# A gated ConvFFN inside a two-layer diffusion backbone: a second tile for the gate chunk, weight sums made in place, a fourth raw buffer, and smaller pieces around them

## The chip, the cores and the metric

The kernel runs on one core of a Trainium2 chip. The metric is the device time of one execution in microseconds (us), lower is better. The kernel before takes 3467.93 us in the median of two runs (3467.13 and 3468.74).

## The reference, cut to what matters

One sequence of 1024 latent tokens (width 1024) and 256 context tokens goes through two layers: differential attention, then neighbourhood attention on a 16 x 64 grid, each followed by the same gated feed-forward block with a three-point convolution along the tokens (D_FF is 2816). Scale, shift and gate of each block come from a modulation matrix `ada_w`. Layer 1 has no context output.

```python
def conv_ffn(t, w_up, w_conv, b_conv, w_down):
    u = t @ w_up                                   # (n, 1024) @ (1024, 5632)
    up = jnp.pad(u, ((0, 0), (1, 1), (0, 0)))
    acc = b_conv
    for tap in range(3):
        acc = acc + up[:, tap:tap + n] * w_conv[tap]
    a, g = jnp.split(acc, 2, axis=-1)
    return (jax.nn.silu(g) * a) @ w_down
...
x = x + g2 * conv_ffn(rmsnorm(x, norm_ffn[i]) * (1.0 + sc2) + sh2, ...)
```

## The kernel before

All large products are fp32 to near full accuracy from a reduced-precision matmul format: every operand is split into a high part and a low remainder, and a product is high x high + high x low + low x high, three matmuls per 128 x 128 block of weights. A weight split is a cast on ScalarE for the high part and a subtraction on GpSimd (POOL) or VectorE (DVE) for the low one.

`Weights` (L75 to L205) is one stream of weight blocks in the order in which the kernel consumes them. It loads raw fp32 tiles of [128, 1024] into a ring of `RAW` = 3 buffers (pool `raw3`, L1141 to L1145), splits them (cast L138, subtraction L142; `high_low` L146 to L151 for weights that are built from others) and hands them out by `get`. SyncE (SP) issues all these DMAs in order.

The up projection of the FFN over the 1024 latent tokens uses a fast scheme with seven products for a 2 x 2 block product (token halves by weight halves), so it needs sums and differences of weight quarters a1, a2, g1, g2 (a and g are the value and gate columns of one chunk of 128 channels) and the token forms T1 to T4 and B22 (`token_forms`, L558 to L598). Each product is 12 matmuls of 512 columns.

- Pass 1 of layer 0 goes over the 22 chunks: the context product for a and g (48 matmuls of 256 columns), and for the first `ne` = 11 chunks also two latent products (`first`, `second`, L617 to L625). For these 11 the sums are built on POOL by `sums` (L180 to L190, four additions in place) and written to DRAM (`sscr`). The token forms are made meanwhile, two steps per chunk from chunk 2 on (loop L660). Layer 1 has no context; its pass 1 runs over 8 chunks.
- The main loop (L686 to L736) goes over all 22 chunks in the order of `SEQUENCE`: chunk ne + i, then chunk i, so 11 pairs in layer 0, and 8 pairs and 6 single chunks in layer 1. A chunk i >= ne is loaded by `pair` (L153) as raw a and g tiles, gets its sums in the loop by `halves` (L159 to L178, which here uses the pool `sum3`), and needs 7 products of 12 matmuls. A chunk i < ne reads its sums back from `sscr` and needs 5 products. So a pair is 144 matmuls.
- What follows each product in the loop is DVE and ScalarE work whose order is written out by hand (PE and DVE are on a manual schedule): additions of two products (L696, L700, L708, L715, L719) give the columns of a and g, ScalarE writes the middle tap (`centre`, L627), DVE adds the other taps (`tap`, L630), ScalarE applies Silu (L727), and `gated` (L730) multiplies and stores to `gscr`. Four such items of a chunk are put in a list `rest` and are run within the next chunk: tap of acc_g, the second tap with Silu, the two taps from `uh`, and gated. `while rest: fill()` before L708 empties the list. The gate chunk `ug` is one tile (`work[:, 3]`), so ug of the next chunk can't be written before acc_g has read it.

The down projection (`down`, L760 onward) runs three blocks of columns in layer 0 (at 0: context, 256 columns; at 1 and at 2: 512 columns each), 22 weight blocks k for each, eight output rows j. At a turn between blocks two weight blocks are taken first for all j (L783 to L797): six of the eight banks are free at once, and the norm of the block before is put in at j = 4 and j = 6. In layer 0 hooks add work beside it: `ada_rows` (L1226 to L1237) multiplies quarters of layer 1's modulation matrix by the conditioning vector on DVE, at the steps of `ADA_AT`; `ada_columns` (L1245) turns the rows by tiny matmuls; at the steps of `SUM_AT` `sums` builds the weight sums of layer 1.

## Time and profile before

| | us |
|---|---|
| median of the runs | 3467.93 |
| the profiled execution | 3468.82 |
| span of the trace of that execution | 3467.0 |
| layer 0 FFN: pass 1, first 11 and other 11 chunks | 156.9 and 63.2 |
| layer 0 FFN: 11 pairs | 439.8 |
| layer 0 FFN: down at 0 and the turn after it; at 1; turn; at 2 | 113.5; 105.9; 30.0; 143.5 |
| layer 1 FFN: pass 1; 8 pairs; 6 single chunks | 40.0; 327.7; 118.8 |
| layer 1 FFN: down of both blocks with the turn | 238.5 |

The span is what the trace covers; 1.8 us lie around it. The stages are windows of the trace cut at the matmuls that begin them. The rest of the span, about 1690 us, is attention and projections.

### The profile page before, as it was taken

Reading aid. Unit: us, or ns where it says so; the run is one execution under the profiler, and the core shown is the slowest. Engines: PE = TensorE matmul, PEld = TensorE weight load, DVE = VectorE, ACT = ScalarE, POOL = GpSimd, SP = SyncE. Lnnn points to the kernel's source line nnn. Section 1 sums busy time; section 2 is a strip of 40 time slices with the busy share of each in tenths; the row PEclk is TensorE's granted clock in tenths of the full one; section 3 lists DMA queues with packets and bytes.
Section 4 is the critical chain, followed back from the end, with each engine's and each line's share of the span. In section 5 each row is a group of like instructions: output and inputs, shape, how many; then the busy total and the mean of one; then the engine's idle time right before and its main releaser. Section 6 shows DMA issues by size and latency. Waiting matters only on the chain.

```text
span 3467.0 us, 43539 instructions
## 1 busy us (share of the span) xinstructions
PE 3192.5 (92%) x15632; PEld 2624.0 (76%) x15632; DVE 2130.6 (61%) x3294; ACT 1400.1 (40%) x2388; POOL 1730.6 (50%) x984
## 2 busy tenths in 40 slices
PE   8999889998998888888989979999999888889998
PEld 4888667776777877777867768888997677778876
DVE  6577488887467466666575344425994766676352
ACT  3111277775143543333423232225993433334111
POOL 2224166663347765555733641113662455678763
PEclk9999999998999999999989999999999999999999
DMA  7565344342445733333665667647873333334542
GB/s 258 161 220 172 107 110 107 111 116 88 152 139 182 216 117 104 116 113 112 231 210 177 213 221 236 224 150 175 197 193 125 123 111 113 109 107 157 196 156 70
DMA packets 253928, 536.82 MB, mean 155 GB/s; under 512 B 29584, under 2 KB 102160, under 8 KB 253712
## 3 DMA queue, kind: packets, MB, share of 16 engines
q1 hardware_dynamic: 252704, 533.72, 48.6%
q8 instruction: 124, 2.03, 0.3%
q14 instruction: 92, 0.75, 0.1%
q10 hardware_dynamic: 1008, 0.32, 0.0%
HBM read 395.24 MB, written 138.67 MB: 154 GB/s over the span
## 4 chain that ended last, share of the span: by engine, by line
PE 49%; POOL 16%; issue 13%; DVE 11%; DMA 8%; ACT 3%; SPq 0%; POOLq 0%; ACTq 0%; DVEq 0%
PE qk_ps L428 9%; PE w_ps L767 9%; POOL wsp L142 6%; PE w_ps L608 6%; POOL wf L151 4%; PE wo_ps L428 3%; PE o L1038 3%; PE sl L987 3%; PE o L1429 2%; PE v_ps L438 2%; PE v_ps L439 2%; PE v_ps L440 2%; PE tp L1014 2%; PE w_ps L428 1%; DMA raw<-in_down_dram 1%
## 5 line engine op out<-in xcount | busy, mean ns | idle before, releaser
L142 POOL TENSOR_TENSOR wsp<-raw,wsp 128x1024 fp32r<-128x1024 f32 (+2 forms) x285 | 647.9, 2281 | 716.6 <-ACT wsp L138 710.8
L767 PE MATMUL w_ps<-g,wsp 128*128 128x512 f32 (+1 forms) x2640 | 575.8, 380 | 50.1 <-POOL wsp L142 23.2
L767 PEld LDWEIGHTS w_ps<-g,wsp 128*128 128x128 f32 x2640 | 474.4, 195 | 150.1 <-POOL wsp L142 28.8
L138 ACT CAST wsp<-raw 128x1024 fp32r<-128x1024 f32 (+1 forms) x213 | 195.0, 928 | 365.1 <-PE w_ps L608 158.2
L608 PE MATMUL w_ps<-FT,wsp 128*128 128x512 f32 x912 | 253.8, 437 | 83.4 <-DVE work L708 58.7
L428 PE MATMUL qk_ps<-Hh,wsp 128*128 128x512 f32 x1280 | 319.7, 372 | 0.0
L140 POOL TENSOR_SCALAR wsp<-raw 128x1024 fp32r<-128x1024 f32 x72 | 99.8, 1388 | 397.4 <-DMA raw<-in_wqk_dram 144.8
L608 PEld LDWEIGHTS w_ps<-FT,wsp 128*128 128x128 f32 x912 | 190.4, 212 | 140.2 <-issue 97.5
L608 PE MATMUL w_ps<-FT,wf 128*128 128x512 f32 x1200 | 288.1, 392 | 4.4 <-DVE t L696 4.3
L608 PEld LDWEIGHTS w_ps<-FT,wf 128*128 128x128 f32 x1200 | 226.5, 189 | 53.9 <-DVE t L696 4.8
L555 DVE TENSOR_TENSOR g<-t,g 128x512 fp32r<-128x512 f32 (+1 forms) x102 | 135.8, 1372 | 211.6 <-ACT g L554 211.6
L428 PEld LDWEIGHTS qk_ps<-Hh,wsp 128*128 128x128 f32 x1280 | 215.3, 188 | 38.2
L630 DVE SCALAR_TENSOR_TENSOR work<-work,c_ffn_conv 128x1023 f32<-128x1023 f32 x88 | 170.9, 1943 | 98.1 <-ACT work L627 97.2
L994 ACT ACTIVATE E<-E,st 128x1280 f32<-128x1280 f32 x128 | 175.4, 1370 | 65.1 <-DVE st L989 64.1
L1004 POOL TENSOR_TENSOR E<-E,E 128x1280 f32<-128x1280 f32 x64 | 188.3, 2943 | 5.3
L608 PE MATMUL w_ps<-Hh,wsp 128*128 128x512 f32 x528 | 177.6, 402 | 8.4 <-ACT p L620 8.4
L1002 POOL TENSOR_SCALAR E<-E,st 128x1280 f32<-128x1280 f32 x64 | 85.6, 1337 | 193.4 <-DVE st L997 122.1
L989 DVE CUSTOM_DVE_ANT_0 E<-sl,zero,st 128x1024 f32<-128x1024 f32 x128 | 163.8, 1281 | 22.9 <-PE sl L987 22.2
L428 PE MATMUL qk_ps<-Hl,wsp 128*128 128x512 f32 (+1 forms) x640 | 175.3, 371 | 0.0
L1366 POOL TENSOR_SCALAR E<-E,st 128x640 f32<-128x640 f32 (+1 forms) x128 | 98.9, 774 | 149.9 <-PE s L1357 81.6
L987 PE MATMUL sl<-kst,q 128*128 128x512 f32 x512 | 160.0, 436 | 1.6 <-DVE st L989 1.5
L352 DVE SCALAR_TENSOR_TENSOR ada<-raw,c_cvec,ada 128x512 f32<-128x512 f32 x168 | 133.0, 827 | 41.2 <-DMA raw<-in_ada_w_dram 39.9
(606 smaller groups left out, 7011.7 us busy)
## 6 DMA issues: line engine op xcount, KB each, us to landing
raw<-in_down_dram SPq DMA_DIRECT2D x110, 512.0 KB
raw<-in_ada_w_dram SPq DMA_DIRECT2D x96, 512.0 KB
gscr<-work SPq DMA_DIRECT2D x44, 512.0 KB
t<-gscr SPq DMA_DIRECT2D x88, 256.0 KB
raw<-sscr SPq DMA_DIRECT2D x38, 512.0 KB
raw<-in_up_dram SPq DMA_DIRECT2D x33, 512.0 KB
raw<-in_wqk_dram SPq DMA_DIRECT2D x32, 512.0 KB
q<-qscr SPq DMA_DIRECT2D x256, 64.0 KB
```

What stands on the lines that cost most here:

```text
L138: nc.scalar.copy(out=sp[:, 0, c:c + n], in_=raw[:, c:c + n])
L142: nc.gpsimd.tensor_tensor(out=sp[:, 1, c:c + n], in0=raw[:, c:c + n], in1=f32(sp[:, 0, c:c + n]), op=ALU.subtract)
L151: nc.gpsimd.tensor_tensor(out=sp[:, 1, :], in0=src, in1=f32(sp[:, 0, :]), op=ALU.subtract)
L428: T.matmul(out=ps, lhsT=w[:, kc, :], rhs=H[b][s][:, kc, :], start=(kc == 0 and i == 0), stop=(kc == KC - 1 and i == 2))
L555: eng.tensor_tensor(out=form[:, kc, 1, :], in0=x, in1=f32(form[:, kc, 0, :]), op=ALU.subtract)
L608: T.matmul(out=ps, lhsT=w, rhs=form(kc, s), start=(start and kc + i == 0), stop=(kc == 3 and i == 2), skip_group_check=not start)
L630: stt(out=acc, in0=u, scalar=convw[:, l, c, k:k + 1], in1=acc, op0=ALU.mult, op1=ALU.add)
L767: T.matmul(out=ys[j][:, :n], lhsT=w[:, j, :], rhs=g[:, k % 4, s, :], start=(k == 0 and i == 0), stop=(k == NF - 1 and i == 2))
L987: T.matmul(out=ps[:, 512 * c:512 * c + 512], lhsT=qs[2 * j + s][:, qc], rhs=ks[j][:, 512 * c:512 * c + 512], start=(s == 0), stop=(s == 1))
L989: V.tensor_tensor_reduce(out=E[j][:, :SEQ], in0=ps, in1=zero.broadcast_to([P, SEQ]), op0=ALU.add, op1=ALU.min, scale=-1.0, scalar=m, accum ...
L994: S.activation(out=E[j], in_=E[j], func=AF.Exp, scale=-1.0, bias=m, accum_out=sm)
L1004: G.tensor_tensor(out=E[0], in0=E[0], in1=E[1], op=ALU.add)
```

## The change

`sums` and the forms of the chunks i >= ne now share one routine, `add_up`, that works in place in the two raw tiles: g2 is split first (`raw.append(self.high_low(g2, 512, False))`), then four additions turn the tiles into the four combinations, then the whole a tile and the whole g tile are split. The pool of the sum tile goes, and the raw ring gets a fourth buffer. The sums are written to DRAM as two tiles instead of four halves, and the main loop takes T1 and T3 from one weight tile, T2 and B22 from the other. `ug` alternates between two tiles, and the last item of `rest` (gated) is run after the addition that writes ug[hi]. Token forms advance one step per chunk in layer 0, and `second` with its copies stands ahead of them. The context product takes its bank from the six-bank pool. The quarters of `ada_w` no longer come through the weight stream: `ada_rows` loads them into a tile of its own, which has the name and the buffer of the second ug tile, and all 16 stand at (at 1, k = 3 to 18). At a turn three weight blocks are taken for j = 0 to 5 before j = 6 and 7. Small ones: `NP1` of layer 1 is 3 and `late` holds two; `R` has one buffer in the last phase; the split tiles of layer 1's q and k share one ring of three.

```diff
-NP1 = (2, 4)
-RAW = 3
+NP1 = (2, 3)
+RAW = 4
-ADA_AT = [(0, 6), (0, 12)] + [(1, k) for k in range(3, 17)]
-SUM_AT = [(2, k) for k in range(2, 18, 2)]
+ADA_AT = [(1, k) for k in range(3, 19)]
+SUM_AT = [(2, k) for k in range(3, 19, 2)]
...
         if i == 0:
-            raw.append(self.sum_pool.tile([P, 1024], F32, name=f"sum{self.count}", tag="sum"))
-            s = raw[2]
-            tt(out=s[:, 512:], in0=g1, in1=g2, op=ALU.add)
-            tt(out=s[:, :512], in0=s[:, 512:], in1=a1, op=ALU.subtract)
+            raw.append(self.high_low(g2, 512, False))
+            self.add_up(a1, a2, g1, g2)
+            self.high_low(ra, 1024)
         elif i == 1:
-            tt(out=a1, in0=a1, in1=g1, op=ALU.subtract)
-            tt(out=a2, in0=a2, in1=raw[2][:, :512], op=ALU.subtract)
-        self.high_low((raw[2], ra, g2)[i] if i < 2 else g2, (1024, 1024, 512)[i])
+            self.high_low(rg, 1024)
+        else:
+            self.made.append((raw[2], 0))
...
-                    gg, ps = W.get(), bank(1)
+                    gg, ps = W.get(), bank()
...
-                for _ in range((2, 99)[l]):
+                for _ in range((1, 99)[l]):
...
-        acc_g, ug = work[:, 2], work[:, 3]
+        acc_g, ug2 = work[:, 2], np_.tile([P, SEQ], F32, name="ug")
...
-                while rest:
+                while len(rest) > 1:
                     fill()
+                acc_a, uh, ug = work[:, at % 2], np_.tile([P, 514], F32, name="uh"), work[:, 3] if at % 2 else ug2
                 V.tensor_tensor(out=ug[:, hi], in0=y, in1=q, op=add)
-                acc_a, uh = work[:, at % 2], np_.tile([P, 514], F32, name="uh")
+                fill()
...
-                for j in range(KC):
-                    if b == 1 and j == 4:
-                        if turn:
-                            turn()
-                        chain = rnorm_steps(yp, np_, SS, 0, 512)
-                        next(chain)
-                    if j == 6:
-                        if b == 1:
-                            write(0, out_[0], next(chain))
-                        ys.extend(bank(1) for _ in range(2))
+                for j in range(6):
                     for k in range(2):
+                        down(k, j, sps[k])
+                if b == 1:
+                    if turn:
+                        turn()
+                    chain = rnorm_steps(yp, np_, SS, 0, 512)
+                    next(chain)
+                sps.append(W.get())
+                load_g(1)
+                for j in range(6):
+                    down(2, j, sps[2])
+                if b == 1:
+                    write(0, out_[0], next(chain))
+                ys.extend(bank(1) for _ in range(2))
+                for j in (6, 7):
+                    for k in range(3):
                         down(k, j, sps[k])
...
-                if l == 0 and (at, k) in ADA_AT:
-                    add_quarters(q1, 1)
...
-        t = W.get().rearrange("p (k n) -> p k n", k=2)
+        t = np_.tile([P, 1024], F32, name="ug")
+        nc.sync.dma_start(out=t, in_=a["ada_w"][1, n, k])
+        t = t.rearrange("p (k n) -> p k n", k=2)
```

ScalarE in the main loop, in the chunk that reads its sums back, before (raw154a, raw154g and sum154 belong to the chunk after it):

```order
L138 CAST wsp153_11938<-raw153_11936 128x1024
L627 ACTIVATE work_11126<-uh_11919,c_ffn_conv_74 128x512
L150 CAST wf154_11968<-sum154_11965 128x1024
L627 ACTIVATE work_11126<-work_11126,c_ffn_conv_74 128x1024
L727 ACTIVATE work_11126<-work_11126 128x1024
L150 CAST wf155_12006<-raw154a_11961 128x1024
L711 COPY uh_12026<-t_11958 128x1
L150 CAST wf156_12043<-raw154g_11962 128x512
L627 ACTIVATE work_11126<-uh_12026,c_ffn_conv_74 128x512
```

The same place in the changed kernel:

```order
L138 CAST wsp153_11910<-raw153_11908 128x1024
L628 ACTIVATE work_11100<-uh_11890,c_ffn_conv_74 128x512
L149 CAST wf154_11937<-raw154g_11934 128x512
L628 ACTIVATE work_11100<-ug_11101,c_ffn_conv_74 128x1024
L731 ACTIVATE work_11100<-work_11100 128x1024
L715 COPY uh_11997<-t_11930 128x1
L149 CAST wf154_11944<-raw154a_11933 128x1024
L149 CAST wf155_11961<-raw154g_11934 128x1024
L628 ACTIVATE work_11100<-uh_11997,c_ffn_conv_74 128x512
```

Ahead of the middle tap of acc_g (the 128x1024 row that reads work or ug) there now stands the cast of g2, which reads the loaded tile, in place of the cast of sum154, which reads a result of POOL; the two casts of built weights come after Silu and the copy to uh.

VectorE in the same chunk, before, from the lower gate half of the chunk ahead (L719) on:

```order
L719 TENSOR_TENSOR work_11126<-w_ps_11853,p1_11833 128x512
L630 SCALAR_TENSOR_TENSOR work_11126<-work_11126,c_ffn_conv_74 128x1023
L696 TENSOR_TENSOR t_11972<-w_ps_11971,p1_11957 128x512
L630 SCALAR_TENSOR_TENSOR work_11126<-work_11126,c_ffn_conv_74 128x1023
L700 TENSOR_TENSOR t_11988<-w_ps_11987,p1_11957 128x512
L630 SCALAR_TENSOR_TENSOR work_11126<-uh_11919,c_ffn_conv_74,work_11126 128x512 x2
L730 TENSOR_TENSOR work_11126<-work_11126 128x1024
L708 TENSOR_TENSOR work_11126<-w_ps_11971,t_11988 128x512
L630 SCALAR_TENSOR_TENSOR work_11126<-t_11958,c_ffn_conv_74,work_11126 128x511
L715 TENSOR_TENSOR uh_12026<-w_ps_11987,t_11972 128x512
L630 SCALAR_TENSOR_TENSOR work_11126<-t_11958,c_ffn_conv_74,work_11126 128x511
L719 TENSOR_TENSOR work_11126<-w_ps_11971,p1_11957 128x512
```

The same in the changed kernel, where that half is L723 and the others are L700, L704, L712 (ug[hi]), L734 (gated) and L719 (uh):

```order
L723 TENSOR_TENSOR ug_11101<-w_ps_11825,p1_11805 128x512
L631 SCALAR_TENSOR_TENSOR work_11100<-ug_11101,c_ffn_conv_74,work_11100 128x1023
L700 TENSOR_TENSOR t_11948<-w_ps_11947,p1_11929 128x512
L631 SCALAR_TENSOR_TENSOR work_11100<-ug_11101,c_ffn_conv_74,work_11100 128x1023
L704 TENSOR_TENSOR t_11967<-w_ps_11966,p1_11929 128x512
L631 SCALAR_TENSOR_TENSOR work_11100<-uh_11890,c_ffn_conv_74,work_11100 128x512 x2
L712 TENSOR_TENSOR work_11100<-w_ps_11947,t_11967 128x512
L734 TENSOR_TENSOR work_11100<-work_11100 128x1024
L631 SCALAR_TENSOR_TENSOR work_11100<-t_11930,c_ffn_conv_74,work_11100 128x511
L719 TENSOR_TENSOR uh_11997<-w_ps_11966,t_11948 128x512
L631 SCALAR_TENSOR_TENSOR work_11100<-t_11930,c_ffn_conv_74,work_11100 128x511
L723 TENSOR_TENSOR work_11100<-w_ps_11947,p1_11929 128x512
```

The product gated and the addition to ug[hi] have changed places; the two taps of acc_g still stand on either side of the first addition.

SyncE's queue in the down projection at 1, before:

```order
L128 DMA raw_14778<-in_down_dram 128x1024
L128 DMA raw_14783<-in_ada_w_dram 128x1024
L754 DMA t<-gscr_10_137 128x512
L128 DMA raw_14817<-in_down_dram 128x1024
L128 DMA raw_14822<-in_ada_w_dram 128x1024
L754 DMA t<-gscr_11_138 128x512
L128 DMA raw_14856<-in_down_dram 128x1024
L754 DMA t<-gscr_12_139 128x512
L754 DMA t<-gscr_13_140 128x512
L128 DMA raw_14861<-in_ada_w_dram 128x1024
```

A like stretch in the changed kernel:

```order
L1238 DMA ug<-in_ada_w_dram 128x1024
L128 DMA raw_14833<-in_down_dram 128x1024
L758 DMA t<-gscr_13_140 128x512
L758 DMA t<-gscr_14_141 128x512
L758 DMA t<-gscr_15_142 128x512
L758 DMA t<-gscr_16_143 128x512
L1238 DMA ug<-in_ada_w_dram 128x1024
L128 DMA raw_14873<-in_down_dram 128x1024
L758 DMA t<-gscr_17_144 128x512
L758 DMA t<-gscr_18_145 128x512
L128 DMA raw_14912<-in_down_dram 128x1024
L1238 DMA ug<-in_ada_w_dram 128x1024
```

The modulation quarters (in_ada_w) were written to tiles of the weight ring, and now to the one tile ug; the down weights and the stored gate products (gscr) still stand between them on the same queue.

## Rows read from the trace of the kernel before

**Rows 1.** The page's first part: busy us, share of span, instructions by engine.

```profile
PE 3192.5 (92%) x15632; PEld 2624.0 (76%) x15632; DVE 2130.6 (61%) x3294; ACT 1400.1 (40%) x2388; POOL 1730.6 (50%) x984
```

**Rows 2.** Windows: stretch, length, busy PE PEld DVE ACT POOL, TensorE clock, DMA, GB/s.

```profile
1220.80:1660.60 439.80, 390.33 (x1586) 312.06 (x1585) 286.54 (x274) 166.92 (x215) 252.71 (x121) 0.93 0.34 113
2753.00:3080.70 327.70, 289.09 (x1188) 232.56 (x1188) 212.18 (x199) 123.53 (x157) 194.30 (x91) 0.95 0.34 114
3080.70:3199.50 118.80, 118.76 (x517) 98.19 (x518) 81.06 (x75) 52.10 (x65) 96.25 (x48) 0.99 0.38 125
1380.10:1385.20 5.10, 5.04 (x12) 4.00 (x13) 2.24 (x3) 0.81 (x1) 0.43 (x1) 0.52 0.65 222
```

**Rows 3.** Waits over the span: engine, line, waited for; total us, times, longest.

```profile
PE w_ps L608 <- DVE work L708: 58.7, 17, 4.3
PE w_ps L608 <- DVE t L696: 29.1, 19, 4.3
```

**Rows 4.** Timeline, layer 0 pairs: start, length, engine, line, operation, idle before, releaser.

```profile
1360.60 2.88 PE L608 MATMUL w_ps<-FT,wf 128*128 128x512 f32 x12
...
1363.32 5.70 PE L608 MATMUL w_ps<-FT,wsp 128*128 128x512 f32 x24
...
1365.89 1.05 ACT L150 CAST wf<-sum 128x1024 fp32r<-128x1024 f32 x1 [3.28 <-POOL sum L174]
...
1368.11 1.28 DVE L630 SCALAR_TENSOR_TENSOR work<-work,c_ffn_conv 128x1023 f32<-128x1023 f32 x1 [3.90 <-ACT work L627]
...
1370.15 3.01 PE L608 MATMUL w_ps<-FT,wsp 128*128 128x512 f32 x12 [1.13 <-DVE t L696]
...
1372.13 4.00 DVE L630 SCALAR_TENSOR_TENSOR work<-uh,c_ffn_conv,work 128x512 f32<-128x512 f32 x2
...
1376.23 3.18 DVE L730 TENSOR_TENSOR work<-work 128x1024 f32<-128x1024 f32 x1
...
1379.33 0.68 DVE L708 TENSOR_TENSOR work<-w_ps,t 128x512 f32<-128x512 f32 x1
...
1380.16 5.24 PE L608 MATMUL w_ps<-FT,wsp 128*128 128x512 f32 x12 [4.29 <-DVE work L708]
...
1391.88 1.53 DVE L630 SCALAR_TENSOR_TENSOR work<-uh,c_ffn_conv,work 128x512 f32<-128x512 f32 x2
...
1394.34 1.22 DVE L730 TENSOR_TENSOR work<-work 128x1024 f32<-128x1024 f32 x1
...
1394.91 2.90 POOL L142 TENSOR_TENSOR wsp<-raw,wsp 128x1024 fp32r<-128x1024 f32 x1 [5.94 <-ACT wsp L138]
```

**Rows 5.** Windows of pass 1 of layer 0: first eleven chunks, other eleven.

```profile
1000.70:1157.60 156.90, 133.57 (x805) 118.82 (x804) 92.62 (x102) 62.26 (x97) 113.39 (x63) 0.95 0.60 193
1157.60:1220.80 63.20, 63.20 (x529) 63.20 (x529) 35.54 (x47) 35.04 (x51) 52.10 (x24) 1.00 0.63 193
```

**Rows 6.** Timeline of one chunk of pass 1, ScalarE and GpSimd.

```profile
1106.41 1.05 ACT L150 CAST wf<-raw97g 128x1024 fp32r<-128x1024 f32 x1 [5.64 <-DMA raw97g<-in_up_dram]
...
1107.54 2.39 POOL L151 TENSOR_TENSOR wf<-raw97g,wf 128x1024 fp32r<-128x1024 f32 x1 [3.41 <-ACT wf L150]
...
1110.00 1.29 POOL L185 TENSOR_TENSOR raw97g<-raw97g 128x512 f32<-128x512 f32 x1
```

**Rows 7.** Windows, layer 0 down: context and turn; at 1; part of at 2.

```profile
1660.60:1774.10 113.50, 91.48 (x597) 83.41 (x597) 64.60 (x70) 41.46 (x62) 68.71 (x29) 0.86 0.71 234
1774.10:1880.00 105.90, 105.50 (x462) 86.27 (x460) 66.52 (x70) 30.76 (x39) 44.06 (x18) 1.00 0.60 201
1960.00:2053.50 93.50, 70.14 (x268) 52.85 (x267) 21.20 (x21) 21.32 (x28) 57.68 (x33) 0.89 0.69 237
```

**Rows 8.** Timeline: a modulation quarter's issue and first use; layer 1's turn.

```profile
1735.94 0.33 SPq L128 DMA_DIRECT2D raw<-in_ada_w_dram  x1
...
1739.84 1.42 DVE L1237 SCALAR_TENSOR_TENSOR rows<-raw,c_cvec,rows 128x512 f32<-128x512 f32 x2 [6.19 <-DMA raw<-in_ada_w_dram]
...
3330.85 1.87 PE L387 MATMUL rn_ps<-mean_w,SS 128*128 128x2 f32 x8 [4.95 <-DVE SS L375]
```

More of the change, by code (lines that the diff above doesn't have):

```diff
@@ L188, in sums @@
         tt(out=a2, in0=a2, in1=a1, op=ALU.subtract)
-        for k, t in enumerate((a1, g2, g1, a2)):
-            nc.sync.dma_start(out=dst[:, 512 * k:512 * k + 512], in_=t)
+    def sums(self, ra, rg, dst):
+        self.add_up(ra[:, :512], ra[:, 512:], rg[:, :512], rg[:, 512:])
+        for k, t in enumerate((ra, rg)):
+            self.nc.sync.dma_start(out=dst[:, 1024 * k:1024 * k + 1024], in_=t)
     def get(self):
@@ L391, in rnorm_steps @@
         V.reciprocal(out=col[:, :nt], in_=col[:, :nt])
-        R = pool.tile([P, 512], F32, name="R", bufs=2)
+        R = pool.tile([P, 512], F32, name="R", bufs=rbufs[0])
         V.tensor_tensor(out=R[:, :n].rearrange("p (t q) -> p t q", q=P), in0=ident.unsqueeze(1).broadcast_to([P, nt, P]),
@@ L653, in ffn @@
                     late.append((i, aa, x, p1))
+                n_late = (1, 2)[l] if i < ne - 1 else 0
+                late, keep = late[:len(late) - n_late], late[len(late) - n_late:] if n_late else []
+                for e, aa, x, p1 in late:
+                    second(x, aa)
+                    c11 = small()
+                    S.copy(out=c11, in_=x)
+                    for k, t in enumerate((p1, c11)):
+                        nc.sync.dma_start(out=escr[l][e][k], in_=t)
+                late = keep
                 if i == 1:
@@ L659, in ffn @@
                     steps = token_forms()
-                for _ in range((2, 99)[l]):
+                for _ in range((1, 99)[l]):
                     if steps and not F.get("rest"):
                         F["rest"] = next(steps)
-                for e, aa, x, p1 in late[:-1] if i < ne - 1 else late:
-                    second(x, aa)
-                    c11 = small()
-                    S.copy(out=c11, in_=x)
-                    for k, t in enumerate((p1, c11)):
-                        nc.sync.dma_start(out=escr[l][e][k], in_=t)
-                late = late[-1:] if i < ne - 1 else []
         finish_all(steps)
         work = xpool.tile([P, 4, SEQ], F32, name="work", tag="X1")
-        acc_g, ug = work[:, 2], work[:, 3]
+        acc_g, ug2 = work[:, 2], np_.tile([P, SEQ], F32, name="ug")
         rest = deque()
@@ L734, in ffn @@
                 centre(acc_g, ug, NF + i)
-                rest.extend((lambda i=i: tap(acc_g[:, 1:], ug[:, :-1], NF + i, 0), end_g, end_a, gated))
+                rest.extend((lambda i=i, ug=ug: tap(acc_g[:, 1:], ug[:, :-1], NF + i, 0), end_g, end_a, gated))
             while rest:
@@ L800, in ffn @@
                         nc.sync.dma_start(out=out_[b][:, c:c + 4, :], in_=xspill[l][:, c:c + 4, b0:b0 + n])
-                for k in range(2, NF - 3):
+                for k in range(3, NF - 3):
                     sp = W.get()
@@ L1144, in _body @@
     W.split_pool = es.enter_context(tc.tile_pool(name="split3", bufs=5, reuse_waits="tile"))
-    W.sum_pool = es.enter_context(tc.tile_pool(name="sum3", bufs=1, reuse_waits="tile"))
     for l in range(2):
@@ L1304, in _body @@
         sums.close()
-        pool = ph.enter_context(tc.tile_pool(name="p5", bufs=1, reuse_waits="tile"))
         na0 = front.enter_context(tc.tile_pool(name="na0", bufs=1, side="right", reuse_waits="tile"))
         first, na_pools[0] = {}, na0
-        his, los = (xpool.tile([P, 3, NT], F32R, name=f"{c}s", tag=f"X{i}", padded_shape=[P, 3, 1365]) for i, c in enumerate(("hi", "lo")))
+        split3, r3 = (xpool.tile([P, 3, NT], d, name=c, tag=f"X{i}", padded_shape=[P, 3, 1365])
+                      for i, (c, d) in enumerate((("split3", F32R), ("r3", F32))))
         for g in range(8):
@@ L1313, in _body @@
                 n_all = sum(BLOCKS[nb - 1])
-                t = pool.tile([P, NT], F32, name="r", bufs=1)
+                t = r3[:, (2 * g + nb) % 3]
                 tp = t[:, :SEQ].rearrange("p (b r c) -> p r b c", b=NB, c=CB)
@@ L1322, in _body @@
                         S.activation(out=t[:, b0:b0 + n], in_=pss[b][:, :n], func=AF.Copy, scale=sc)
-                hi, lo = (x[:, (2 * g + nb) % 3] for x in (his, los))
+                hi, lo = (split3[:, (2 * (2 * g + nb) + x) % 3] for x in range(2))
                 S.copy(out=hi[:, :n_all], in_=t[:, :n_all])
```

24 lines of the change are left out of this document (12 added, 12 removed).

## Prediction

> **What bounds the kernel now.** I read the page's first part, then windows cut by stage, then the waits, then the timeline of one chunk. TensorE (PE) is busy 92% of the span [rows 1], so the whole can shrink only where PE stands still or runs at a low clock. The windows show where the FFN does that: the single chunks of layer 1 leave nothing (118.76 busy of 118.80), the pairs leave 49.5 us in layer 0 and 38.6 in layer 1 [rows 2]. The waits name it: 58.7 us for the addition that writes ug[hi] (L708), 17 times, and 29.1 for L696, 19 times [rows 3].
>
> How a pair comes to its length: 12 matmuls take 2.72 us (1360.60 to 1363.32, rows 4), so its 144 need 32.64. The 11 pairs take 439.8/11 = 39.98 each, the 8 pairs of layer 1 327.7/8 = 40.96 [rows 2]. In all, 80.7 + 66.6 = 147 us are lost. The timeline shows the cause, in the chunk with stored sums that begins at 1363.32. ScalarE's cast of `sum` at 1365.89 has waited 3.28 us for POOL, and the middle tap of acc_g stands behind it, so DVE's first tap waits 3.90 us and starts at 1368.11. From there DVE is one chain: taps, L696 (PE waits 1.13), taps from uh 4.00, gated 3.18, and only then L708 at 1379.33. PE waits 4.29 us, and the 12 matmuls behind it take 5.24 instead of 2.72 [rows 4]: the granted clock of that stretch is 0.52 [rows 2], about the 1.2 GHz level, where it was full before the wait. So the place costs 1.13 + 4.29 + 2.5 = 7.9 us, against 39.98 - 32.64 = 7.3 for the mean pair. That is the whole loss.
>
> **The change part by part.** The sum is made against the profiled execution's own 3468.8 us (span 3467.0, 1.8 around it); the median of the runs is 0.9 lower.
>
> Main loop. I replay the chunk at 1363.32 in the new order. The cast ahead of the middle tap is now of g2, half as wide, and waits for a transfer instead of POOL; the addition L719 is done at 1364.2 as before, so the middle tap ends near 1365.5 instead of 1368.1: 2.6 us earlier. Tap 1.28, first addition 0.68 (done at 1367.5, before PE's next product is due at 1368.8, so the 1.13 goes), tap 1.7, second addition 0.68, uh taps 4.00: 1373.9. Gated now stands behind ug[hi], which is written by 1374.6. PE finishes the two products before at 1374.2 (1363.32 + 4 x 2.72). So with the durations of this row PE waits 0.4 us. Four additions now run on POOL where before there were two, a split and two, so DVE's taps are likelier to lie beside them; I add 1 to 2 us for that: wait 0.4 to 2.4. A wait of 1.13 left the 12 matmuls behind it at 3.01 [rows 4], so the low clock should mostly go too. Gated's 3.18 now lies in front of L719 and L723, which nobody on PE waits for soon: the next chunk begins with two products into other banks, 5.4 us. I take 1.4 for the wait, and 1.4 for pairs where the clock still falls or POOL hands over late: 35.4 per pair. Saved: 4.6 x 11 + 5.6 x 8 = 95 us. The ends: no wait left (33.0 per pair) gives 141; a wait of 3.4 with half of the slow stretch left and 2 us lost elsewhere (39.0) gives 27.
>
> In-place sums. POOL per pair: 5 full splits, 2 half ones, 4 additions, before and after; the work is the same (252.71/11 = 23.0 us per pair, rows 2), only its order is new. The chain is longer: split of g2, four additions, split of a, against two additions and a split. From 1363.2 (raw g landed) that is 1.3 + 4 x 1.3 + 2.4 = 8.9 alone, perhaps 13.5 beside DVE. PE needs the first built weight after 6 products, at 1379.6 at the earliest, so 3 to 7 us are over: 0. That is a cover: if the transfer of g came 5 us later, it would be on the path.
>
> Pass 1 of layer 0. 11 chunks take 156.9/11 = 14.3 us each with PE busy 133.57/11 = 12.1 [rows 5]. POOL does a split (2.39), four additions (1.29 each) and a split, some 10.5, and then stands 3.4 us for the cast of the next raw g, which waited 5.64 us for its transfer [rows 6]: with three raw buffers the g tile can't be loaded until the sums are written out. A fourth buffer lets pairs alternate. The bound is then PE's 12.1, so up to 2.2 x 11 = 24 us; the token forms at one step per chunk take DVE work from the first eleven chunks and put it beside the other eleven, where PE has no idle time and DVE 63.2 - 35.5 = 27.7 [rows 5]. It fits if no more than that moves, and costs up to 10 if not. The bank of the context product, and `second` ahead of the forms, go with this. I take -12, range -25 to +5.
>
> Down projection. Context block and turn: PE is busy 91.48 of 113.5, clock 0.86 [rows 7]; the fourth raw buffer lets POOL run further ahead, and two modulation quarters leave the stream: -8 (0 to -20). At 1: 105.50 of 105.90 is PE, nothing to gain; the 16 quarters now go through one tile. A quarter's cycle is transfer 3.9 (1735.94 to 1739.84) plus four operations of 0.71 (1.42 for two, rows 8), 2.8, plus its place in DVE's queue, 1: about 8 us, 16 x 8 = 128 against 105.9 for the stage, so the quarters run on into the next turn. The down weights stand between them on the same queue, but the ring of four is ahead of PE: I take 0, range -3 to +40. At 2, with the sums of layer 1: 70.14 busy of 93.5, clock 0.89 [rows 7]; a pair tile now waits less for the ring: -8 (0 to -20). Six banks first at a turn: PE gets 54 matmuls instead of 36 before it needs the norm, for which it waits 4.95 us in layer 1 [rows 8]: 18 x 0.23 = 4.1 of it can go, in both layers: -4 (0 to -10). What is late next there is the addition into the last two banks.
>
> The rest. Layer 1's pass 1 with two chunks late and three p1, and the one R buffer: -1 (-5 to +5, by the wait of 4.95, the nearest row). The shared ring for q and k of layer 1 adds a wait on a buffer where PE has no idle: 0 (+5).
>
> Sum: -95 - 12 - 8 + 0 - 8 - 4 - 1 + 0 = -128: 3468.8 - 128 = 3341.
>
> **A rule that speaks against this.** The same DVE operations take 1.53 (two uh taps) and 1.22 (gated) at 1391.88 and 1394.34, where POOL stands idle until 1394.91, and 4.00 and 3.18 beside POOL [rows 4]. The Trainium skill says it in "SBUF — State Buffer", section "Who interferes with whom": a VectorE instruction with two inputs in SBUF contends with a GpSimd instruction that reads SBUF, through a shared pair of ports held exclusively. The trace agrees. Taken strictly, the two engines' work adds up, which is the first rival below.
>
> **The rivals.**
> Rival 1, the shared port is the bound. Work alone per pair: DVE 4 long taps x 1.28 + 6 short x 0.77 + 2 gated x 1.22 = 12.2; POOL 5 x 2.39 + 2 x 1.2 + 4 x 1.29 = 19.5; together 31.7, against PE's 32.64. So it fits only if neither ever waits for another engine. For it: 4.00 against 1.53. Against it: in layer 1's single chunks the two are busy 81.06 + 96.25 us in 118.8 and PE never stops [rows 2]. If it holds, all four taps stand behind additions at twice their time, the wait before T4 is 3 us and its clock still falls: 32.64 + 3 + 2.5 = 38.1 per pair, saving 1.8 x 11 + 2.8 x 8 = 42. With the other terms at 24 (pass 1 gains less, POOL being fuller): 3468.8 - 66 = 3403.
>
> Rival 2, the other side: the one modulation tile stops SyncE's queue. Each of the 16 transfers stands in order before down weights and gate products (the rows of SyncE above), and waits for the four DVE operations on the quarter before, which stand in DVE's queue behind work that waits for just those gate products. If the loop closes, one step k takes transfer 3.9, DVE 2.8, then the weight's transfer 3.9, cast and split 3.4, 24 matmuls 5.44: 19.4 instead of 5.44. The whole is slower than before if a cycle lasts over 5.44 + 128/16 = 13.4 us; half way between, at 16.4, it costs 16 x 11 = 175 and the time is 3341 + 175 = 3516. Against it: a ring of four holds four steps, 22 us of PE, while a quarter needs 8.
>
> Rival 3, the saving is there but half: the wait moves to the next product as POOL's longer chain hands the first built weight over 3 us late in each pair (its slack was 3 to 7, with raw g landing when it does now). 19 x 3 = 57 less: 3398. It speaks for it that gated's store, on which SyncE's queue waits, is moved.
>
> That the change doesn't do what it says is small: the order lists show both gated behind ug[hi] and the g2 cast ahead of the middle tap.
>
> **How the numbers follow.** Forecast 0.70, rival 1 0.13, rival 3 0.10, rival 2 0.04, the rest (other mishaps to about no change) 0.03. The forecast's own range is 3341 - 45 (main loop 141, rest the same) to 3341 + 50, so 3296 to 3391. The range for 8 in 10 takes in rivals 1 and 3: 3292 to 3412. A measurement tells 2% from no change here, 69 us: faster means below 3398.6, slower above 3537 us. Faster: nearly all of the forecast (0.68 of 0.70), half of rival 3 (0.05), a third of rival 1 (0.05) and 0.02 of the rest: 0.80. Slower by over 2% is the larger part of neither side: a third of rival 2 lies above 3537, and 0.01 for others: 0.03. Within 2% the rest: 0.17. The time is 3341.
>
> **What would show it.** Right: in the waits, L608 for the ug[hi] addition falls from 58.7 to below 20; the loop windows become 389 and 283 us with a clock near 1; the first tap of acc_g starts 2.6 us earlier in its chunk; pass 1's first part is near 145; at 1 stays near 106. Wrong: the 12 matmuls of T4 still at 5 us (rival 1), PE waiting for the split of the built a tile (rival 3), PE idle for down weights at 1 while SyncE waits for ug (rival 2).

## The result, and the profile after

The changed kernel takes 3301.92 us in the median of two runs (3301.09 to 3302.75), against 3467.93: a ratio of 0.9521, 95% interval 0.948 to 0.9562, so 166 us less. The forecast was 3341 with a range of 3292 to 3412: the direction and the place are right, the gain was put 38 us too low.

The page's first part of the changed kernel, the row that answers to [rows 1]:

```profile
PE 3139.8 (95%) x15632; PEld 2597.7 (79%) x15632; DVE 2141.8 (65%) x3294; ACT 1397.1 (42%) x2388; POOL 1750.4 (53%) x984
```

TensorE has the same 15632 matmuls and is busy 53 us less, since more of them ran at the full clock; 113 us of idle time went. Where, the starts of the stages in both traces say (a stage runs from its first matmul to the next one's; us):

| stage | before | after | difference | forecast |
|---|---|---|---|---|
| layer 0, pass 1 | 220.1 | 202.0 | -18.1 | -12 |
| layer 0, 11 pairs | 439.9 | 364.8 | -75.1 | -50 |
| layer 0, down at 0, turn, at 1 | 220.2 | 216.2 | -4.0 | -8 |
| layer 0, second turn and at 2 | 172.8 | 162.1 | -10.7 | -10 |
| layer 1, pass 1 | 63.6 | 54.2 | -9.4 | -1 |
| layer 1, 8 pairs | 319.2 | 271.7 | -47.5 | -45 |
| layer 1, 6 single chunks | 114.2 | 118.2 | +4.0 | 0 |
| layer 1, down from the norm on | 119.4 | 116.8 | -2.6 | -2 |
| all else | | | -2.6 | 0 |

Layer 1's windows ahead of the prediction were cut elsewhere: its pass 1 begins at 2702.4 and takes 63.6 us, not 40.0, and its down projection takes 250.8 from the first matmul to the last, not 238.5. In the experiments the down projection of layer 0 is cut at the tiny matmuls of `ada_columns` in the second turn, where the changed kernel has 230.5 us before them and 147.8 from them on. For the kernel before that cut gives 231.5 and 161.5, which can't be set against it: 24 matmuls of at 2 stood ahead of the tiny ones, and now 36 do.

The table of windows of the changed kernel, columns as in [rows 2], to be read against [rows 2, 5, 7]. In order: the first eleven chunks of pass 1 of layer 0; its pairs; the context block with its turn; in layer 1 the first pair, the other seven, the single chunks.

```profile
999.50:1138.10 138.60, 129.41 (x803) 116.73 (x802) 98.61 (x102) 62.05 (x98) 117.47 (x63) 0.96 0.65 218
1201.50:1566.30 364.80, 362.20 (x1586) 296.83 (x1585) 278.15 (x273) 168.16 (x214) 261.32 (x119) 1.00 0.42 139
1566.30:1680.00 113.70, 89.64 (x616) 82.78 (x615) 75.57 (x70) 41.67 (x62) 68.39 (x30) 0.91 0.67 219
2646.40:2689.60 43.20, 36.17 (x146) 28.90 (x145) 23.19 (x23) 18.88 (x26) 31.37 (x17) 0.88 0.33 106
2689.60:2918.00 228.40, 228.40 (x1009) 189.15 (x1008) 175.48 (x169) 102.99 (x127) 169.09 (x78) 1.00 0.42 138
2918.00:3036.30 118.30, 115.67 (x507) 94.26 (x506) 76.85 (x71) 47.82 (x64) 88.43 (x47) 1.00 0.36 119
```

Seven pairs of layer 1 take 228.4 us with TensorE busy throughout at the full clock. By the starts of their matmuls each takes 32.64, the figure that the prediction worked out for a pair without a wait. Layer 0's take 32.8 after a first one of 36.5, in which DVE is still making the last token form and TensorE waits 2.27 us for L700. The waits of [rows 3], 58.7 and 29.1 us, are gone from the list; what is left for the FFN's products is this:

```profile
PE w_ps L609 <- ACT p L621: 10.1, 3, 5.0
PE w_ps L609 <- ACT wf L149: 5.8, 1, 5.8
PE w_ps L609 <- POOL wf L150: 3.8, 5, 1.2
PE w_ps L609 <- DVE t L700: 2.3, 1, 2.3
```

The timeline of a chunk with stored sums in the changed kernel, rows as in [rows 4]:

```profile
1355.62 8.41 PE L609 MATMUL w_ps<-FT,wsp 128*128 128x512 f32 x36
...
1355.82 0.62 ACT L149 CAST wf<-raw161g 128x512 fp32r<-128x512 f32 x1 [0.95 <-PE w_ps L609]
...
1356.61 1.25 ACT L628 ACTIVATE work<-ug,c_ffn_conv 128x1024 f32<-128x1024 f32 x1 [0.17 <-DVE ug L723]
...
1357.89 1.28 DVE L631 SCALAR_TENSOR_TENSOR work<-ug,c_ffn_conv,work 128x1023 f32<-128x1023 f32 x1 [1.37 <-ACT work L628]
...
1361.96 2.86 DVE L631 SCALAR_TENSOR_TENSOR work<-uh,c_ffn_conv,work 128x512 f32<-128x512 f32 x2
...
1362.65 1.62 POOL L184 TENSOR_TENSOR raw161a<-raw161g,raw161a 128x512 f32<-128x512 f32 x1
...
1364.74 0.68 DVE L712 TENSOR_TENSOR work<-w_ps,t 128x512 f32<-128x512 f32 x1
...
1365.35 1.72 DVE L734 TENSOR_TENSOR work<-work 128x1024 f32<-128x1024 f32 x1
...
1366.59 2.88 PE L609 MATMUL w_ps<-FT,wsp 128*128 128x512 f32 x12
```

The cast of g2 waits for no result of POOL, the middle tap has waited only 0.17 us for its input, and the first tap starts 2.27 us into the chunk instead of 4.79 [rows 4]. Three products run without a stop. The addition into ug[hi] ends near 1365.4 and T4 begins at 1366.59, so some 1.2 us are to spare; gated comes behind it.

### The profile page after: what moved, and what is told of

The parts are those of the page before. It is cut to its first block, busy times and chain, and to the rows that moved or that the text cites. A ratio compares the mean times of both kernels' runs of the same rounds, so it can differ in the third digit from the quotient of the medians.

```text
span 3301.0 us, 43509 instructions
## 1 busy us (share of the span) xinstructions
PE 3139.8 (95%) x15632; PEld 2597.7 (79%) x15632; DVE 2141.8 (65%) x3294; ACT 1397.1 (42%) x2388; POOL 1750.4 (53%) x984
## 3 DMA queue, kind: packets, MB, share of 16 engines
q1 hardware_dynamic: 247232, 533.71, 50.9%
## 4 chain that ended last, share of the span: by engine, by line
PE 65%; DVE 11%; POOL 9%; issue 7%; DMA 5%; ACT 3%; SPq 0%; ACTq 0%; POOLq 0%; DVEq 0%
PE w_ps L609 21%; PE qk_ps L429 10%; PE w_ps L771 7%; POOL wsp L142 4%; PE wo_ps L429 3%; PE o L1048 3%; PE sl L997 2%; PE v_ps L440 2%; PE o L1438 2%; PE v_ps L439 2%; PE v_ps L441 2%; PE tp L1024 2%; PE w_ps L429 2%; DVE E L999 1%; POOL wf L150 1%
## 5 line engine op out<-in xcount | busy, mean ns | idle before, releaser
L142 POOL TENSOR_TENSOR wsp<-raw,wsp 128x1024 fp32r<-128x1024 f32 (+2 forms) x285 | 666.2, 2345 | 669.2 <-ACT wsp L138 570.4
L771 PE MATMUL w_ps<-g,wsp 128*128 128x512 f32 (+1 forms) x2640 | 568.6, 377 | 40.7 <-POOL wsp L142 14.6
L771 PEld LDWEIGHTS w_ps<-g,wsp 128*128 128x128 f32 x2640 | 471.4, 193 | 136.5 <-POOL wsp L142 17.8
L556 DVE TENSOR_TENSOR g<-t,g 128x512 fp32r<-128x512 f32 (+1 forms) x102 | 144.2, 1459 | 185.7 <-ACT g L555 183.1
L609 PE MATMUL w_ps<-FT,wsp 128*128 128x512 f32 x912 | 214.0, 390 | 0.0
L609 PEld LDWEIGHTS w_ps<-FT,wsp 128*128 128x128 f32 x912 | 171.1, 188 | 36.7 <-DVE t L700 0.2
L353 DVE SCALAR_TENSOR_TENSOR ada<-raw,c_cvec,ada 128x512 f32<-128x512 f32 x168 | 135.5, 840 | 36.7 <-DMA raw<-in_ada_w_dram 35.4
L1048 PE MATMUL o<-T,vt 128*128 128x512 f32 (+1 forms) x464 | 154.2, 460 | 0.6 <-ACT ot L1055 0.5
```

The lines of the kernel that those rows point to most:

```text
L142: nc.gpsimd.tensor_tensor(out=sp[:, 1, c:c + n], in0=raw[:, c:c + n], in1=f32(sp[:, 0, c:c + n]), op=ALU.subtract)
L353: stt(out=accs[v], in0=tv[:, kk, :], scalar=scol[:, kc, v:v + 1], in1=accs[v], op0=ALU.mult, op1=ALU.add)
L556: eng.tensor_tensor(out=form[:, kc, 1, :], in0=x, in1=f32(form[:, kc, 0, :]), op=ALU.subtract)
L609: T.matmul(out=ps, lhsT=w, rhs=form(kc, s), start=(start and kc + i == 0), stop=(kc == 3 and i == 2), skip_group_check=not start)
L771: T.matmul(out=ys[j][:, :n], lhsT=w[:, j, :], rhs=g[:, k % 4, s, :], start=(k == 0 and i == 0), stop=(k == NF - 1 and i == 2))
L1048: T.matmul(out=o[:, :n], lhsT=w, rhs=x, start=(i == 0 and j == 0), stop=(i == len(seq) - 1 and j == len(three) - 1))
```

## The experiments

Each kernel is the changed one with the edit shown. Ratios are against runs of the kernel before on the same chip; pairs and stages are read from starts of matmuls in each trace.

**1. Gated back in its old place.**

```diff
-                while len(rest) > 1:
+                while rest:
                     fill()
...
-                fill()
```

> The changed kernel with gated put back ahead of the addition that writes ug[hi]. Theory of the chain (both edits take time out of one DVE chain): in the changed kernel the addition ends 1.16 us before T4's matmuls begin, and gated there takes 1.7 us (3.2 beside POOL), so TensorE waits 0.6 to 2.0 us per pair and the pairs go from 32.8 to about 34 us with the clock still near full: 19 x 1.2 = 23 us more, about 3325. Rival (the place of gated is what the main loop gained by): the waits of 4 us and the low clock come back, 38 to 40 us per pair, about 3400 to 3430.

3325.19 us, ratio 0.9593 (0.9565 to 0.9621). Pairs: 34.1 in layer 0 (39.4 the first, 32.9 the last), 34.0 to 34.6 in layer 1 after a first one of 47.1. The wait and one of its places:

```profile
PE w_ps L609 <- DVE work L712: 21.0, 18, 2.2
```

```profile
1372.82 2.12 DVE L733 TENSOR_TENSOR work<-work 128x1024 f32<-128x1024 f32 x1
...
1374.87 0.68 DVE L712 TENSOR_TENSOR work<-w_ps,t 128x512 f32<-128x512 f32 x1
...
1375.69 3.00 PE L609 MATMUL w_ps<-FT,wsp 128*128 128x512 f32 x12 [1.03 <-DVE work L712]
```

Gated takes 2.12, eats the slack and leaves 1.03 us of waiting, 21.0 in all. The loops are 29 us longer and the whole 23, since stages that the edit doesn't touch came out shorter (230.5 to 226.9 in layer 0's down, 116.8 to 113.6 in layer 1's). The 12 matmuls behind the wait take 3.00, so the clock stays. The theory of the chain holds; the place of gated is worth 1.3 to 1.4 us per pair here, no more.

**2. Weight sums as before, three raw buffers** (old `halves` and `sums`, sum tile, old order of the weight tiles; gated in its new place).

```diff
-RAW = 4
+RAW = 3
...
-            raw.append(self.high_low(g2, 512, False))
-            self.add_up(a1, a2, g1, g2)
-            self.high_low(ra, 1024)
+            raw.append(self.sum_pool.tile([P, 1024], F32, name=f"sum{self.count}", tag="sum"))
...
+        self.high_low((raw[2], ra, g2)[i] if i < 2 else g2, (1024, 1024, 512)[i])
```

> The changed kernel with the weight sums as before (sum tile of its own, cast of the sum ahead of the middle tap, sums written as four halves) and three raw buffers, gated still behind ug[hi]. Theory of the chain: the middle tap is 2.6 us late again, so TensorE waits about 1.1 us for T3 and 1.4 us for T4 per pair: 35.3 us per pair, 48 us more in the loops, and some 18 us more in pass 1 and down at 2 for the third buffer: about 3368. Rival (the place of gated alone): pairs stay at 32.8, about 3320.

3427.06 us, ratio 0.9883 (0.9859 to 0.9907), 59 us above the expected time. Layer 0's pairs take 415.7 us, 37.8 each, layer 1's 308.3. Waits and one place:

```profile
PE w_ps L610 <- DVE t L700: 49.6, 19, 4.6
```

```profile
1396.81 5.70 PE L610 MATMUL w_ps<-FT,wsp 128*128 128x512 f32 x24
...
1398.27 1.29 POOL L175 TENSOR_TENSOR sum<-raw161g 128x512 f32<-128x512 f32 x1 [5.07 <-DMA raw161g<-in_up_dram]
...
1403.20 2.40 DVE L632 SCALAR_TENSOR_TENSOR work<-ug,c_ffn_conv,work 128x1023 f32<-128x1023 f32 x1 [5.50 <-ACT work L629]
...
1406.34 2.04 PE L610 MATMUL w_ps<-FT,wsp 128*128 128x512 f32 x4 [3.84 <-DVE t L700]
```

The rival falls: gated's place alone doesn't free the pair. The mechanism is the one named (transfer of g, two additions, cast of the sum, middle tap, tap), but it acts on T3, a product earlier than most of it was expected, and costs nearly twice as much (50.9 + 36.6 us in the loops, 48 expected). The first addition, which waits for the transfer of g, starts 1.46 us after the chunk begins, so the first tap waits 5.50 us. In the kernel before it started 0.13 us ahead of the chunk, which began at 1363.32 [rows 4]:

```profile
1363.19 1.29 POOL L173 TENSOR_TENSOR sum<-raw154g 128x512 f32<-128x512 f32 x1 [5.22 <-DMA raw154g<-in_up_dram]
```

Most of the main loop's gain (87.5 of 122.5 us) is the order of the weight sums together with the ring; this run undoes both.

**3. Three raw buffers, sums in place.**

```diff
-RAW = 4
+RAW = 3
```

> The changed kernel with three raw buffers in place of four. Theory (the fourth buffer lets pairs alternate): pass 1 of layer 0 goes back from 138.6 to about 157 us, down at 2 by about 10 us, and the pairs lose 0 to 2 us each since a pair now holds two of three buffers until its last split: 3330 to 3370, about 3345. Rival (the gain of pass 1 came from the slower pace of the token forms): pass 1 stays near 139, whole time within 10 us of 3302.

3379.09 us, ratio 0.9744 (0.972 to 0.9768): 77 us more, and 9 above the range that was expected; pass 1 and at 2 lost more than I had put. Pass 1 of layer 0 takes 229.5 (more than before's 220.1), second turn and at 2 165.5, layer 0's pairs 33.6 to 34.9 each after a first one of 40.0, the last 32.9. POOL in pass 1, first in this kernel, then in the changed one:

```profile
1096.12 2.41 POOL L150 TENSOR_TENSOR wf<-raw95g,wf 128x1024 fp32r<-128x1024 f32 x1 [3.64 <-ACT wf L149]
```

```profile
1082.27 1.30 POOL L182 TENSOR_TENSOR raw95g<-raw95g 128x512 f32<-128x512 f32 x1
...
1087.66 2.58 POOL L150 TENSOR_TENSOR wf<-raw97a,wf 128x1024 fp32r<-128x1024 f32 x1
1090.20 2.84 POOL L150 TENSOR_TENSOR wf<-raw97g,wf 128x1024 fp32r<-128x1024 f32 x1
```

With three buffers POOL stands 3.64 us before the split of g, as before [rows 6]; with four it goes from the split of a to that of g without a stop. The fourth buffer is 27.5 us of pass 1, 17.8 of at 2, and 1.3 per pair. In pass 1 that is more than the 18.1 us that the stage gained in all: with three buffers the other edits lose there. Experiment 2, which has three buffers too but writes the sums as four halves, takes 222.5. From 2 and 3 together: with three buffers the in-place sums bring a pair from 37.8 to about 34, the buffer another 1.3.

**4. One ug tile.**

```diff
-        acc_g, ug2 = work[:, 2], np_.tile([P, SEQ], F32, name="ug")
+        acc_g = work[:, 2]
...
-                acc_a, uh, ug = work[:, at % 2], np_.tile([P, 514], F32, name="uh"), work[:, 3] if at % 2 else ug2
+                acc_a, uh, ug = work[:, at % 2], np_.tile([P, 514], F32, name="uh"), work[:, 3]
```

> The changed kernel with one ug tile for all chunks. Theory: all DVE reads of ug stand ahead of its next write on DVE's own queue, and ScalarE's middle tap is long done, so the second tile carries nothing: 3302, within 5 us, pairs at 32.8. Rival (the second tile is needed for the new order): the addition waits for readers, 1 us or more per pair, 3320 or more.

3301.76 us, ratio 0.9521 (0.9498 to 0.9544), pairs at 32.8 and 32.6: the second tile carries nothing in the pairs; it only lends its buffer to the modulation.

**5. Three edits undone, in three stages.**

```diff
-                for _ in range((1, 99)[l]):
+                for _ in range((2, 99)[l]):
...
-                n_late = (1, 2)[l] if i < ne - 1 else 0
+                n_late = (1, 1)[l] if i < ne - 1 else 0
...
-                for j in range(6):
+                for j in range(KC):
+                    if b == 1 and j == 4:
...
```

> The changed kernel with three edits undone, each in a stage of its own. (a) Token forms two steps per chunk in layer 0: if DVE's load in the first eleven chunks is part of what pass 1 gained, its 138.6 us become about 148; if the fourth buffer alone did it, they stay. (b) Layer 1's pass 1 with one chunk late instead of two: if that removed the wait of 8.4 us for ScalarE's copy of p, the stage goes from 54 to about 62 us; if the in-place sums did, it stays. (c) The turns as before (two weight blocks first, norm at j = 4): the last down of layer 1 from its norm on goes up by 4 us (TensorE waits for the norm again), the one of layer 0 by some 4. By the first readings the time is about 3324, by the second ones 3302 to 3306.

3308.84 us, ratio 0.9541 (0.9526 to 0.9555). (a) Pass 1 of layer 0 takes 206.0 against 202.0: between the two readings, the slower pace is worth 4 us. (b) Pass 1 of layer 1 goes to 56.9, but its first pair from 43.2 to 33.7: two chunks late lose 9.5 us in the pair. They seem to gain 2.8 in the stage, but experiment 8, with the same edit, has 53.2 there, so that gain isn't firm. Both readings fell; the edit is a loss. (c) In layer 1 the last down takes 119.5 from the norm on against 116.8: TensorE waits 4.96 us for the norm, as before [rows 8], where it waits 2.27 in the changed kernel:

```profile
3167.79 1.72 PE L388 MATMUL rn_ps<-mean_w,SS 128*128 128x2 f32 x8 [2.27 <-DVE SS L376]
3169.37 6.90 PE L771 MATMUL w_ps<-g,wsp 128*128 128x512 f32 x18
```

Experiment 1 has 113.6 there with the changed code and a wait of 2.26. Its 18 matmuls behind the wait take 4.38 at a granted clock of 1.00, where these take 6.90 (0.50 from 3169.4 to 3173.4). So six banks first are worth 2.7 us in layer 1, and up to 5.9 where the clock stays.

In layer 0 the old turn costs nearly nothing in the second turn: at 2 takes 162.7 from its first matmul on, against 161.9 to 162.3 in the changed kernel and experiments 1 and 4. It costs in the first turn, which I had left out. From the context block's last matmul to at 2's first one it is 149.4, against 141.8 to 145.9 in the changed kernel and experiments 1, 4 and 8, so six banks first gain 3.5 to 7.6 there. TensorE's waits for L780, the additions that free the last banks, are 6.4 us in that stretch against 0.8 to 2.7 in the other four.

**6. Three quarters of the modulation left out.**

```diff
-            ada_rows(i // 4, i % 4)
+            if i % 4 == 0:
+                ada_rows(i // 4, i % 4)
```

> The changed kernel with 12 of the 16 modulation quarters of layer 1 left out (neither loaded nor multiplied). Theory: their DVE operations stand in the turn after the context block ahead of the splits of g, for which TensorE waits 8.8 and 5.1 us there, so the stretch from the down projection's start to the tiny matmuls falls from 230.5 to about 220 us and the time to about 3292. Rival: the turn is set by the loads of X and g, and the stretch stays within 2 us.

3296.58 us, ratio 0.951 (0.9494 to 0.9526). The kernel leaves out 12 of the 16 quarters, so only its time is of use. From the start of down to the tiny matmuls it takes 221.7 us, near the 220 expected, against 230.5 in the changed kernel. But experiments 1, 4 and 8, which have the same code there, take 226.9, 226.2 and 224.0, so the effect is 2.3 to 8.8 us, and it isn't the one named. The changed kernel's turn, DVE and then TensorE:

```profile
1648.85 5.43 DVE L1246 SCALAR_TENSOR_TENSOR rows<-ug,c_cvec,rows 128x512 f32<-128x512 f32 x3 [1.44 <-DMA ug<-in_ada_w_dram]
...
1654.60 2.48 DVE L556 TENSOR_TENSOR g<-t,g 128x512 fp32r<-128x512 f32 x4
```

```profile
1649.41 0.79 PE L771 MATMUL w_ps<-g,wsp 128*128 128x512 f32 x1 [8.76 <-ACT g L555]
1655.33 8.73 PE L771 MATMUL w_ps<-g,wsp 128*128 128x512 f32 x29 [5.13 <-DVE g L556]
```

The same in this kernel:

```profile
1642.78 4.38 DVE L1244 TENSOR_SCALAR rows<-ug,c_cvec 128x512 f32<-128x512 f32 x2 [1.30 <-DMA ug<-in_ada_w_dram]
1647.09 1.40 DVE L1246 SCALAR_TENSOR_TENSOR rows<-ug,c_cvec,rows 128x512 f32<-128x512 f32 x2
...
1648.81 2.48 DVE L556 TENSOR_TENSOR g<-t,g 128x512 fp32r<-128x512 f32 x4
```

```profile
1643.47 0.79 PE L771 MATMUL w_ps<-g,wsp 128*128 128x512 f32 x1 [10.11 <-ACT g L555]
1649.53 20.69 PE L771 MATMUL w_ps<-g,wsp 128*128 128x512 f32 x77 [5.27 <-DVE g L556]
```

In the changed kernel the split of g on which TensorE waits 5.13 us stands behind three modulation operations of 5.43. But here it still stands behind four of 5.78 and TensorE waits as long: the four quarters that are left come first, 7.1 us ahead of the down projection's start and 55 to 73 behind it, at about the times of the changed kernel's first four. So this run doesn't price the modulation in the turn; experiment 9 does.

**7. Three new edits.**

```diff
-        for k, t in enumerate((ra, rg)):
+        for k, t in ((1, rg), (0, ra)):
...
-                for _ in range((1, 99)[l]):
+                for _ in range((1, 3)[l]):
...
-ADA_AT = [(1, k) for k in range(3, 19)]
+ADA_AT = [(0, k) for k in range(3, 19)]
```

> The changed kernel with three new edits, each for a stage of its own. (a) sums writes the g tile, which is final after the second addition, ahead of the a tile: buffers free 2.6 us earlier; pass 1 of layer 0 gains 0 to 5 us, down at 2 gains 0 to 8. (b) Token forms three steps per chunk in layer 1 instead of all at once: POOL's split of g2 no longer lies behind a row of DVE splits (5.3 us instead of 1.3), so the first pair of layer 1 falls from 43.2 to 37 to 39 us; rival: DVE is late with the forms instead, and it stays at 43 or more. (c) All modulation quarters at the context block (at 0) instead of at 1: the turn gains up to 10 us; rival: the context block, which moves 240 GB/s, loses as much. Together about 3286; if the rivals hold, 3300 to 3310.

3339.64 us, ratio 0.9633 (0.9618 to 0.9647), slower than the changed kernel. (a) Pass 1 202.6, unchanged; second turn and at 2 143.5, 4.3 less. (b) First pair of layer 1 43.3: no effect, a miss; the split of g2 still lies beside the same nine DVE splits. (c) 268.4 us instead of 230.5: SyncE's queue now waits for the tile,

```profile
SPq L1238 <- DVE rows L1246: 54.7, 12, 11.4
```

with DVE's modulation between the splits of g. The mechanism of rival 2, at another place: 38 us.

**8 and 9. Toward a better version.** First, one chunk late and the g tile written first (the edits of 5 (b) and 7 (a)); then also the modulation through the ring of small tiles:

```diff
-        t = np_.tile([P, 1024], F32, name="ug")
-        nc.sync.dma_start(out=t, in_=a["ada_w"][1, n, k])
...
+            t = small()
+            nc.sync.dma_start(out=t, in_=a["ada_w"][1, n, k][:, 512 * kk:512 * kk + 512])
...
```

> The changed kernel with one chunk late instead of two in layer 1's pass 1, and the g tile of the sums written ahead of the a tile. From the stage of the earlier run: pass 1 of layer 1 with its first pair 97.4 to about 90.6 us; down at 2 with the sums 0 to 4 us less (143.5 stood against 147.8, where the modulation was elsewhere too). About 3293; if the order of the writes carries nothing, 3295; if the late chunk was not the cause, 3302.

> As e_best1, with each modulation quarter of layer 1 loaded as two halves into the ring of small tiles (which the gate products use too) instead of the one tile, so that its turn comes in program order after the context block's turn. Theory: the 9 us that the modulation cost in the turn go, from 230.5 to about 222 us, time about 3284. Rival: in the ring the quarters hold up the gate products of at 1, where TensorE has no idle time, and the stretch stays at 230 or grows, 3293 or more.

3289.55 us, ratio 0.9494 (0.9472 to 0.9516), and 3285.67 us, ratio 0.9473 (0.945 to 0.9496). Pass 1 of layer 1 with the first pair goes from 97.4 to 88.2 and 92.9. From the start of down to the tiny matmuls: 230.5, 224.0, 216.9; in this stage experiment 8 has the changed kernel's code, so its 224.0 is no gain of an edit. In the turn of the last kernel TensorE starts at 1 like this:

```profile
1642.97 0.79 PE L771 MATMUL w_ps<-g,wsp 128*128 128x512 f32 x1 [3.68 <-ACT g L555]
...
1647.27 43.09 PE L771 MATMUL w_ps<-g,wsp 128*128 128x512 f32 x179 [1.14 <-DVE g L556]
```

Waits of 3.68 and 1.14 stand for 8.76 and 5.13 (10.73 and 5.13 in experiment 8), since no quarter is loaded before 93.8 us after the start of down. From the context block's last matmul to at 2's first it takes 134.2 us, against 141.8 to 145.9 in the changed kernel and experiments 1, 4 and 8: the early modulation costs 7.6 to 11.7 us. The rival falls. Second turn and at 2, with the g tile written first, take 143.3 and 146.3 against 147.8. The last kernel is the fastest of the study and clear of the kernel before. The intervals of 8 and 9 overlap with each other and with the changed kernel's (0.948 to 0.9562), so the lead over it rests on the stages.

Not taken apart are the bank of the context product, `second` ahead of the forms, `NP1`, the one R buffer and the shared ring of q and k.

## Why the prediction was right, and where it was off

**Main loop: right in mechanism, under-sized.** The replay put the middle tap 2.6 us earlier (2.5 measured), T3's wait at zero (zero), and ug[hi] written 11.3 us into the chunk (9.8 measured). The term that failed is the allowance for DVE beside POOL: "I take 1.4 for the wait, and 1.4 for pairs where the clock still falls". Both are 0, and uh's taps take 2.86 where I kept 4.00: what runs beside them now is an addition of 1.62, not a split of 2.85, which was this row of the kernel before:

```profile
1372.73 2.85 POOL L151 TENSOR_TENSOR wf<-sum,wf 128x1024 fp32r<-128x1024 f32 x1
```

The pair is 32.6 to 32.8 instead of 35.4, which is 25 us more in layer 0. In layer 1 the total is near by luck: the pairs came out 2.8 us shorter than the 35.4 I put. Against that I had counted 40.96 per pair from a window that held 13 us of pass 1 and lacked the last 4.5 of the pairs (they take 39.9 each), and the first pair cost 10.5 us that I had not.

**Clock: right.** The windows show 1.00 in the pairs where 0.93 and 0.95 stood [rows 2]; a wait of 1.03 (experiment 1) left it there, waits of 4 had brought it to 0.52. A wait of about 2.3 did either: 0.50 behind 2.27 in the changed kernel, 1.00 behind 2.26 in experiment 1 (experiment 5).

**In-place sums cost nothing: right in 17 pairs, wrong at the edges.** The cover of 3 to 7 us that I named is used up in layer 1's first pair and in its last four single chunks (20.0 instead of 19.0). In the single chunks there is no pair's second half to hide the longer chain:

```profile
3000.23 0.33 SPq L158 DMA_DIRECT2D raw417g<-in_up_dram  x1
...
3000.26 5.32 PE L609 MATMUL w_ps<-FT,wf 128*128 128x512 f32 x22 [0.66 <-POOL wf L150]
...
3008.34 0.62 ACT L149 CAST wf<-raw417g 128x512 fp32r<-128x512 f32 x1 [0.21 <-PE w_ps L609]
```

TensorE waits 0.66 us for the split of the built g tile. The next chunk's cast of g2 comes 8.1 us after its transfer's issue, when ScalarE has done Silu and TensorE has given a split buffer back. That was rival 3, at five places instead of nineteen. With the old sums (experiment 2) all six single chunks take 19.0. I had looked at the pair alone.

**Pass 1 of layer 0: right, low by 6.** The reason held (27.5 us by experiment 3, of which the stage's other edits take part back), the token forms cost nothing in the other eleven chunks (63.3 before and after), and their pace gained 4 of its own (experiment 5), which I had as a possible cost.

**Down: sum near, parts other than put.** Context block and turn were put at -8. With at 1 they gave 4.0 in the changed kernel, and 7.6 to 9.8 in experiments 1, 4 and 8, which have the same code there. Two effects that I hadn't counted met in that turn. Six banks first gained 3.5 to 7.6 (experiment 5). The modulation cost 7.6 to 11.7 (experiment 9): I had it "at 1", where the code puts it, and its transfers and operations were issued as soon as tile and rows were free. At 2 with its turn was put at -10 and gave 10.7. Of the wait for the norm in layer 1 I let 4.1 us go, and 2.7 went (4.95 to 2.27): ahead of the norm's matmul there stand 36 matmuls instead of 24, and the 54 and 36 that I counted end at the addition behind it.

**Layer 1's pass 1: not seen.** I put -1; the stage gave 9.4 and took 10.5 back in the first pair. Experiments 2 and 3, which both have three buffers and differ by the weight sums, take 60.5 and 52.9 there, so most of the gain belongs to the in-place sums. Experiment 5 shows one late chunk as the better choice.

**Rivals.** The shared port as bound (1) fell: DVE and POOL are busy 175.5 + 169.1 us in 228.4 of seven pairs and TensorE never stops. Rival 2 didn't happen at 1 and did when the modulation was put at 0 (experiment 7).

## What to carry to other kernels

Replay the engine's queue that stands between two products, row by row, and take only durations whose neighbours will be the same; an allowance on top should be paid for by a row. Look at the first and the last turn of a loop apart from its middle, since what the middle hides lies open there. Where the order is not written by hand, an operation of these kernels runs when its buffer is free, not where the loop calls it: to hold one back, give it a buffer of the ring that paces the loop. Leaving work out prices it only if what is left no longer stands in the same place: look at the wait itself, not at the time alone.
